# Hybrid trunk: the second query tile loaded and split ahead of the second HGRN, its loads and query factors in other places

## The chip, the cores and the metric

The kernel runs on one core of a Trainium2 chip. The time is that of one execution on the device in microseconds (us), median of several runs. The engines are TensorE (PE in the profile, its weight loads PEld), VectorE (DVE), ScalarE (ACT), GpSimd (POOL) and SyncE (SP), which issues all DMAs of this kernel. Each engine works through its own queue in order; semaphores tie them together.

## The reference

Two layers over x, 1024 tokens by 1024 columns, all in float32:

```
h = rms_norm(x);  z = h @ w_in[l]        # 2560 columns, split among three mixers
o_att = attention(q_a, k_a, v_a)         # 8 query heads, 2 key/value heads of 64, QK norm, rotary
o_hg  = hgrn2_bidirectional(...)         # 4 heads with 64 x 64 state, gated recurrence both ways
o_cv  = conformer_conv(a_c, g_c)         # gated, depthwise, 31 taps, layer norm, swish
x = x + concat[o_att, o_hg, o_cv] @ w_out[l]
x = x + relu(rms_norm(x) @ w1[l])^2 @ w2[l]
```

Attention is softmax(q k^T / 8) v without a mask, over all 1024 keys.

## The kernel before, in words

The kernel is written as one long Python program against a tile framework. The framework allots buffers (`tmp` has 4, `x8` has 8, PSUM banks `c`, `e` have 2 each and `S` 2 pairs), adds the semaphores, and orders the instructions of each engine: it goes by the order in which the code is written, but lets an instruction go ahead where its own estimate says that an earlier one isn't ready. So a statement that is moved can also move its neighbours. All arrays stand with columns on partitions and tokens along the free axis. Products need more precision than one fp32r pass, so operands are split into a rounded part and a remainder (ACT copies, DVE or POOL subtracts) and multiplied in three passes.

Within a layer, the mixers run interleaved. A projection of one 128-column tile is `dense_steps` (L227): 48 matmuls of 128x512 into a pair of `S` banks, then an evacuation by DVE (`evac`, L329 and L331). The weights come through `wtile`: a load to `raw` (L200), ACT's copy to `whi` (L203), the remainder to `wlo` by DVE, or by POOL for w_out (L204). First come the convolution's inputs and the first HGRN half (`Hgrn(0)`) with the q, k and v projections (`qkv`); normed and rotated queries and keys go out to DRAM as `qd` and `kd`. The queries' norm factors are only multiplied in later, by `query_norm(j)`, for all but the first of four: it loads 512 KB of qd, widens the factors `nqc` over the tokens (ACT, L172, into a `tmp` buffer), turns them by PE transposes (L182), multiplies (DVE, L676) and stores.

Then the attention's first steps are woven into the second HGRN half, `h1 = Hgrn(1, mid)`: its constructor does five projections (q, two forget gates, the output gate, and the value i), and `mid` is called ahead of the last. Its output gate is stored to DRAM (`gd`, L443), and its core is a generator, `gen`, advanced inside the attention loop. In the same projections ends the convolution (`cg`), whose outputs go to `mixd` (L409).

Attention goes over 16 query tiles `w` (head h, half of the tokens: 512 queries). For one tile:
- `att_query(w)` loads 64 rows of qd twice (L769, two DMAs of 128 KB), copies them on ACT (L774, L775) and subtracts the remainder (L777; on DVE for tile 0, on POOL for the others);
- `att_max(w, i)`, i = 0 to 3: two matmuls of 128x512 against the keys (L785) and two reductions to row maxima on DVE (L788);
- `att_shift(w)`: the maxima of the halves are joined (L791), transposed (L793) and put into the query tile (L794), so that the second pass of the scores subtracts them;
- `att_scores(w, i)`: eight score matmuls by pairs (L807, L808) and the Exp on ACT (L809);
- `att_values(w)`: 64 matmuls (L819) and the division (L827, L828); `att_out(w)` transposes (L841).

`keys(g)` loads and splits the keys of one kv head (L751 to L757). The pool `att` holds the query tiles `Q`, the probabilities `PT` and outputs, and lies in the space that `xs`, the normed input of the projections, frees when the last projection has been read.

## Time and profile before

| | us |
|---|---|
| median of 3 runs | 2493.56 (2493.47 to 2499.18) |
| profiled execution | 2494.11 |
| its span, first to last instruction | 2492.3 |
| PE busy | 2403.3 |
| DVE, ACT, POOL busy | 1832.8, 1070.0, 553.6 |
| mean granted clock of TensorE | 0.982 |

The last projection of the second HGRN ends at about 301 us in layer 0 and 1544 us in layer 1, and the attention loop follows to about 530 and 1773. A timeline row shows the start, the time (of the whole row, where it merges xN instructions), engine, line and operation, and in brackets the idle time before it with what ended it. A row of waits shows who waited for whom, the sum, how often, and the longest.

### The profile page before, as it was taken

How to read it: one execution, taken by the hardware profiler on the slowest of the kernel's cores; microseconds unless marked ns; L12 is line 12 of the kernel's file. 1: busy time of each engine (PE TensorE's matmuls, PEld its weight loads, DVE VectorE, ACT ScalarE, POOL GpSimd, SP SyncE). 2: the span in 40 equal slices, each digit the busy share in tenths (PEclk: the TensorE clock that was granted, in tenths of full speed). 3: DMA queues.
4: the chain of work that ended last, by engine and by line, in shares of the span. 5: the costliest groups of instructions: out<-in, count | busy, mean ns of one | idle time of the engine just before them, and what ended most of it. 6: DMA issues, size and time to landing. Idle time of an engine off the chain costs nothing. (4 is left out here: it accounts for less than half of the span.)

```text
span 2492.3 us, 40044 instructions
## 1 busy us (share of the span) xinstructions
PE 2403.3 (96%) x16192; PEld 1925.2 (77%) x16192; DVE 1832.8 (74%) x2747; ACT 1070.0 (43%) x1616; POOL 553.6 (22%) x305
## 2 busy tenths in 40 slices
PE   8989899999999999999999898999999999999999
PEld 7767667778788887888887676677787888878887
DVE  6998486633977768987859974865349776789886
ACT  5233455543544444433523234555435444444332
POOL 0251432013035420000123424310130354100000
PEclk9999999999999999999999889999999999999999
DMA  4111321042344458444221123210423444574442
GB/s 159 59 35 65 103 81 36 10 153 81 118 151 146 162 178 295 150 172 161 70 101 49 35 73 106 69 36 10 153 85 120 151 162 147 200 270 163 149 152 93
DMA packets 114825, 293.45 MB, mean 118 GB/s; under 512 B 11600, under 2 KB 11984, under 8 KB 114640
## 3 DMA queue, kind: packets, MB, share of 16 engines
q1 hardware_dynamic: 114640, 290.90, 33.4%
q8 instruction: 127, 2.08, 0.3%
q14 instruction: 58, 0.48, 0.1%
HBM read 200.67 MB, written 90.18 MB: 117 GB/s over the span
## 5 line engine op out<-in xcount | busy, mean ns | idle before, releaser
L227 PE MATMUL S<-xs,whi 128*128 128x512 f32 x1280 | 364.1, 404 | 8.4 <-ACT whi L203 7.0
L227 PEld LDWEIGHTS S<-xs,whi 128*128 128x128 f32 x1280 | 242.0, 192 | 62.9 <-ACT whi L203 7.0
L788 DVE TENSOR_REDUCE mq<-c 128x1 f32<-128x512 f32 x256 | 170.5, 685 | 48.1 <-PE c L785 44.0
L1255 PE MATMUL S<-xs,xs 128*128 128x512 f32 x816 | 201.7, 390 | 2.6 <-DVE xs L956 2.6
L227 PE MATMUL S<-xs,wlo 128*128 128x512 f32 x640 | 202.1, 397 | 0.0
L955 ACT ACTIVATE xs<-m 128x512 fp32r<-128x512 f32 x216 | 126.0, 619 | 141.9 <-DVE m L966 50.8
L809 ACT ACTIVATE PT<-S 128x1024 f32<-128x1024 f32 x128 | 128.3, 1023 | 126.1 <-PE S L808 77.8
L1255 PEld LDWEIGHTS S<-xs,xs 128*128 128x128 f32 x816 | 152.9, 188 | 35.5 <-DVE xs L956 3.5
L361 DVE SCALAR_TENSOR_TENSOR x<-x,par,x 128x1014 f32<-128x1014 f32 (+14 forms) x120 | 161.6, 1381 | 0.0
L956 DVE TENSOR_TENSOR xs<-m,xs 128x512 fp32r<-128x512 f32 x216 | 144.8, 693 | 22.5 <-ACT xs L955 22.5
L203 ACT ACTIVATE whi<-raw 128x1024 fp32r<-128x1024 f32 x56 | 59.1, 1057 | 208.4 <-PE S L227 181.5
L227 PEld LDWEIGHTS S<-xs,wlo 128*128 128x128 f32 x640 | 122.4, 192 | 26.3
L819 PEld LDWEIGHTS e<-x,PT 128*64 128x64 f32 x4096 | 124.8, 138 | 22.1 <-issue 9.9
L1255 PE MATMUL e<-xs,xs 128*128 128x512 f32 x552 | 140.8, 390 | 1.0 <-ACT xs L955 0.6
L1255 PE MATMUL c<-xs,xs 128*128 128x512 f32 x552 | 139.2, 389 | 0.0
L819 PE MATMUL e<-x,PT 128*64 128x65 f32 x4096 | 131.4, 223 | 7.6 <-DVE Q L794 3.9
L265 POOL TENSOR_TENSOR tmp<-tmp,tmp 128x1024 f32<-128x1024 f32 x19 | 50.8, 2673 | 363.2 <-ACT tmp L264 363.0
L227 PE MATMUL S<-mx,whi 128*128 128x512 f32 x448 | 122.9, 396 | 0.0
L1255 PEld LDWEIGHTS e<-xs,xs 128*128 128x128 f32 x552 | 103.3, 188 | 24.2 <-DVE xs L956 1.4
L553 POOL TENSOR_TENSOR X<-X,T 128x512 f32<-128x512 f32 x56 | 99.5, 1796 | 96.9 <-ACT m L494 47.2
L1255 PEld LDWEIGHTS c<-xs,xs 128*128 128x128 f32 x552 | 103.6, 188 | 21.5
L785 PE MATMUL c<-x,Q 128*128 128x512 f32 x240 | 101.7, 456 | 14.6 <-POOL Q L777 13.7
(311 smaller groups left out, 5229.1 us busy)
## 6 DMA issues: line engine op xcount, KB each, us to landing
m<-ad SPq DMA_DIRECT2D x104, 512.0 KB, 3.9
ad<-x SPq DMA_DIRECT2D x176, 256.0 KB, 2.2
raw<-w_in_t SPq DMA_DIRECT2D x40, 512.0 KB, 3.3
xs<-w_t SPq DMA_DIRECT2D x36, 512.0 KB, 3.7
raw<-w_t SPq DMA_DIRECT2D x36, 512.0 KB, 3.4
m<-w_t SPq DMA_DIRECT2D x32, 512.0 KB, 6.7
ad<-tmp SPq DMA_DIRECT2D x48, 256.0 KB, 2.2
x<-w_t SPq DMA_DIRECT2D x24, 512.0 KB, 5.0
```

The lines of the kernel that those rows point to most:

```text
L203: nc.scalar.activation(hi, raw, AF.Copy)
L227: nc.tensor.matmul(zp[h] if type(zp) is list else zp[:, h, :], w, xx[:, h * 512 : (h + 1) * 512], start=first, stop=last)
L265: return i, eng.tensor_tensor(self.ssq, self.ssq, sq, op=ALU.add)
L361: nc.vector.scalar_tensor_tensor(y[:, lo:hi], u[:, lo + d : hi + d], par[:, l, wof + tap : wof + tap + 1], y[:, lo:hi], op0=ALU.mult, op1= ...
L553: eng.tensor_tensor(xv, xv, tv, op=ALU.mult)
L785: nc.tensor.matmul(b, QS[w][:, 0, i * P : (i + 1) * P], KH[g][:, hb * 512 : (hb + 1) * 512], start=True, stop=True)
L788: nc.vector.tensor_reduce(MX[w][:, hb, i : i + 1], b, axis=AX.X, op=ALU.max)
L809: nc.scalar.activation(PT[w][:, 2 * i : 2 * i + 2, :], s, AF.Exp)
L819: nc.tensor.matmul(pvp[64 * b : 64 * b + 64, i * 65 : (i + 1) * 65], PT[w][:, kb, q0 : q0 + 64], VS[g][:, kb, 0:65], start=kb == 0, stop=k ...
L955: ordered("a", nc.scalar.activation(hi, src, AF.Copy))
L956: ordered("v", nc.vector.tensor_tensor(lo, src, hi.bitcast(F32), op=ALU.subtract))
L1255: nc.tensor.matmul(banks[dt], w[i][:, dt * P : (dt + 1) * P], a[j], start=n == 0 and name not in ("M6", "M7", "M3"), stop=n == 3 * SG - 1, ...
```

## The change

`att_query(1)` now stands right after `keys(0)`, ahead of the second HGRN, with an `x8` buffer and the subtraction on DVE, as tile 0 has it. `mid` does all four steps of tile 0's maxima ahead of the value projection, no longer two of them. The loads of tiles 2 and up go into two buffers `qq` of their own, in the `att` pool, no longer into `tmp`. The first shift is written ahead of tile 2's load. In the loop, the load of tile w + 3 moves from the head of a pass behind its second scores, and the query factors of passes 0, 2 and 6 behind its fourth.

```diff
         def att_query(w):
             h, half = quads[w]
-            qq = tmp((P, 512))
+            qq = tmp((P, 512)) if w < 2 else ap_.t([P, 512], "qq", bufs=2)
...
-            q = x8((P, 2, 512), dt=F32R) if w == 0 else ap_.t([P, 2, 512], "Q", bufs=4, dt=F32R)
+            q = x8((P, 2, 512), dt=F32R) if w < 2 else ap_.t([P, 2, 512], "Q", bufs=4, dt=F32R)
...
-            eng = nc.gpsimd if w > 0 else nc.vector
+            eng = nc.gpsimd if w > 1 else nc.vector
...
         att_query(0)
         keys(0)
-        h1 = Hgrn(1, lambda: (att_max(0, 0), att_max(0, 1)))
+        att_query(1)
+        h1 = Hgrn(1, lambda: [att_max(0, i) for i in range(4)])
...
         nc.vector.memset(mxw, 0.0)
-        att_query(1)
-        att_max(0, 2)
-        att_max(0, 3)
+        att_shift(0)
         att_query(2)
-        att_shift(0)
...
             if w == 2:
                 keys(1)
-            if w in (0, 2, 6):
-                query_norm((w + 2) // 4 + 1)
-            if w + 3 < NQ:
-                att_query(w + 3)
             for i in range(4):
...
                 if i == 1 and w > 1:
                     att_out(w - 2)
+                if i == 1 and w + 3 < NQ:
+                    att_query(w + 3)
+                if i == 3 and w in (0, 2, 6):
+                    query_norm((w + 2) // 4 + 1)
```

What it does to the engines' queues is the same in both layers; the rows are those of layer 0. In the names `x_259` is query tile 0 (`x_265` tile 1 after), `x_262` and `x_263` are the keys, `c` and `S` PSUM banks.

PE, in the last projection of the second HGRN, before:

```order
L785 MATMUL c_2317<-x_262_1962,x_259_1954 128x512
L227 MATMUL S_314_2333<-xs_103,whi_2132 128x512 x2
L227 MATMUL S_314_2333<-xs_104,whi_2132 128x512 x2
L227 MATMUL S_314_2333<-xs_103,wlo_2133 128x512 x2
L227 MATMUL S_314_2333<-xs_108,whi_2132 128x512 x2
L785 MATMUL c_2320<-x_262_1962,x_259_1954 128x512
L227 MATMUL S_314_2333<-xs_109,whi_2132 128x512 x2
L785 MATMUL c_2323<-x_262_1962,x_259_1954 128x512
```

and after:

```order
L785 MATMUL c_2331<-x_262_1962,x_259_1954 128x512
L227 MATMUL S_321_2353<-xs_108,wlo_2141 128x512
L785 MATMUL c_2334<-x_262_1962,x_259_1954 128x512
L227 MATMUL S_321_2353<-xs_108,wlo_2141 128x512
L227 MATMUL S_321_2353<-xs_113,whi_2140 128x512
L785 MATMUL c_2337<-x_262_1962,x_259_1954 128x512
L227 MATMUL S_321_2353<-xs_113,whi_2140 128x512
L227 MATMUL S_321_2353<-xs_114,whi_2140 128x512
L785 MATMUL c_2340<-x_262_1962,x_259_1954 128x512
```

The second four maxima matmuls of tile 0 follow the first four inside the projection, with one or two of its matmuls between them.

PE, from the end of that projection to the first finished scores (L808), before:

```order
L785 MATMUL c_2397<-x_262_1962,x_259_1954 128x512
L785 MATMUL c_2400<-x_262_1962,x_259_1954 128x512
L807 MATMUL S_336_2447<-x_259_1954,x_262_1962 128x512
L807 MATMUL S_339_2459<-x_259_1954,x_262_1962 128x512
L785 MATMUL c_2403<-x_262_1962,x_259_1954 128x512
L785 MATMUL c_2406<-x_262_1962,x_259_1954 128x512
L785 MATMUL c_2453<-x_262_1962,Q_2392 128x512
L785 MATMUL c_2456<-x_262_1962,Q_2392 128x512
L785 MATMUL c_2465<-x_262_1962,Q_2392 128x512
L793 MATMUL e_2418<-cons_77,mxw_2387 128x128
L182 MATMUL e_2425<-cons_77,tmp_2423 128x128 x4
L785 MATMUL c_2468<-x_262_1962,Q_2392 128x512
```

and after:

```order
L807 MATMUL S_329_2422<-x_259_1954,x_262_1962 128x512
L785 MATMUL c_2428<-x_262_1962,x_265_1970 128x512
L785 MATMUL c_2431<-x_262_1962,x_265_1970 128x512
L807 MATMUL S_332_2434<-x_259_1954,x_262_1962 128x512
L785 MATMUL c_2440<-x_262_1962,x_265_1970 128x512
L793 MATMUL e_2410<-cons_77,mxw_2407 128x128
L182 MATMUL e_2487<-cons_77,tmp_2485 128x128 x4
L785 MATMUL c_2443<-x_262_1962,x_265_1970 128x512
L808 MATMUL S_329_2422<-x_259_1954,x_263_1963 128x512
```

The four matmuls against tile 1 stay ahead of L808, but read the tile that was split ahead of the HGRN; of the two sets of four transposes (L182) one is left there, the other stands behind the first two scores.

ACT, around the same place, before:

```order
L440 ACTIVATE mx_2309<-tmp_2307 128x1
L172 ACTIVATE tmp_2423<-nqc_784 128x1024
L203 ACTIVATE whi_5109<-raw_5107 128x1024
L774 ACTIVATE Q_2392<-tmp_2389 64x512
L775 ACTIVATE Q_2392<-tmp_2389 64x512
L774 ACTIVATE Q_2412<-tmp_2409 64x512
L775 ACTIVATE Q_2412<-tmp_2409 64x512
L774 ACTIVATE Q_2441<-tmp_2438 64x512
L775 ACTIVATE Q_2441<-tmp_2438 64x512
L809 ACTIVATE PT_2446<-S_336_2447 128x1024
```

and after:

```order
L440 ACTIVATE mx_2317<-tmp_2315 128x1
L172 ACTIVATE tmp_2485<-nqc_784 128x1024
L203 ACTIVATE whi_5109<-raw_5107 128x1024
L774 ACTIVATE Q_2416<-qq_2413 64x512
L775 ACTIVATE Q_2416<-qq_2413 64x512
L774 ACTIVATE Q_2449<-qq_2446 64x512
L809 ACTIVATE PT_2421<-S_329_2422 128x1024
```

Ahead of the first Exp stand three query copies in place of six, now those of tiles 2 and 3 out of `qq`; the widened factors (L172) keep their place.

## The prediction

> **What bounds the kernel now.** I read the page's engine lines first, then the waits of TensorE (PE) in the attention stage of each layer (289 to 520 us and 1520 to 1790 us), then the timelines of PE, ScalarE (ACT), GpSimd (POOL) and VectorE (DVE) around the longest wait. PE carries the kernel:

> ```profile
> span 2492.3 us, 40044 instructions
> PE 2403.3 (96%) x16192; PEld 1925.2 (77%) x16192; DVE 1832.8 (74%) x2747; ACT 1070.0 (43%) x1616; POOL 553.6 (22%) x305
> ```

> PE stands still for 89 us in all, so an edit to the order can gain only there. The longest wait of either attention stage is one and the same place, POOL's split of query tile 1 (L777), once in each layer:

> ```profile
> PE c L785 <- POOL Q L777: 7.2, 1, 7.2
> ...
> PE c L785 <- POOL Q L777: 6.5, 1, 6.5
> ```

> The PE timeline of layer 0 shows it between the last projection of the second HGRN (its last rows start at 300.79) and the first finished scores (L808):

> ```profile
> 299.89 1.07 PE L227 MATMUL S<-xs,whi 128*128 128x512 f32 x4
> 300.79 0.62 PE L227 MATMUL S<-xs,wlo 128*128 128x512 f32 x2
> 301.25 0.62 PE L785 MATMUL c<-x,x 128*128 128x512 f32 x2
> ...
> 302.73 0.50 PE L807 MATMUL S<-x,x 128*128 128x512 f32 x1 [0.64 <-DVE m L331]
> 303.41 1.09 PE L785 MATMUL c<-x,x 128*128 128x512 f32 x2 [0.18 <-DVE mq L788]
> 311.74 1.22 PE L785 MATMUL c<-x,Q 128*128 128x512 f32 x2 [7.24 <-POOL Q L777]
> ...
> 315.41 0.72 PE L182 MATMUL e<-cons,tmp 128*128 128x128 f32 x4
> 315.88 0.48 PE L808 MATMUL S<-x,x 128*128 128x512 f32 x1
> ```

> POOL isn't the root. It waited for ACT, and ACT for a store:

> ```profile
> 293.43 0.21 ACT L440 ACTIVATE mx<-tmp 128x1 f32<-128x1 f32 x1
> 305.93 1.05 ACT L172 ACTIVATE tmp<-nqc 128x1024 f32<-128x1024 f32 x1 [12.29 <-DMA gd<-tmp]
> 306.89 1.04 ACT L203 ACTIVATE whi<-raw 128x1024 fp32r<-128x1024 f32 x1
> 307.83 0.61 ACT L774 ACTIVATE Q<-tmp 64x512 fp32r<-64x512 f32 x1
> ...
> 316.85 1.95 ACT L809 ACTIVATE PT<-S 128x1024 f32<-128x1024 f32 x2 [1.02 <-PE S L808]
> ...
> 308.01 2.34 POOL L204 TENSOR_TENSOR wlo<-raw,whi 128x1024 fp32r<-128x1024 f32 x1 [5.86 <-ACT whi L203]
> 310.43 2.49 POOL L777 TENSOR_TENSOR Q<-tmp,Q 64x512 fp32r<-64x512 f32 x2
> ```

> L172 widens the query factors into a tmp buffer that the gate's store still read; ACT is in order, so the weight split (L203) and the query copies (L774) stood behind it, and on POOL the 2.34 us weight split ahead of the query's. After the wait PE also ran slowly: two L785 rows took 1.22 us, where four L227 rows took 1.07. The granted clock (the column before the last two) says why:

> ```profile
> 306.00:308.00 2.00, 0.00 (x0) 0.00 (x0) 0.00 (x0) 2.00 (x3) 0.00 (x0) 0.50 0.12 47
> ...
> 316.00:318.00 2.00, 2.00 (x12) 1.45 (x10) 2.00 (x4) 1.15 (x2) 1.21 (x1) 1.00 0.00 0
> ```

> So the place costs more than the 7.24 us of waiting.

> **The change, priced in layer 0.** Query tile 1 and the second half of tile 0's maxima go ahead of and into the projections.

> *Early load and split.* SP gets two 128 KB loads ahead of three w_out loads, ACT two copies (0.63 us each), DVE one subtraction (0.69), POOL loses one. They sit where these engines are idle:

> ```profile
> 256.05 0.69 DVE L777 TENSOR_TENSOR x<-tmp,x 64x512 fp32r<-64x512 f32 x1 [0.63 <-ACT x L775]
> ...
> 262.35 1.06 ACT L203 ACTIVATE whi<-raw 128x1024 fp32r<-128x1024 f32 x1 [1.56 <-PE S L227]
> ...
> 262.80 1.22 DVE L331 TENSOR_TENSOR tmp<-S,Rb 128x1024 f32<-128x1024 f32 x1 [1.71 <-PE S L227]
> ...
> DMA to landing us min/median/max: 2.4/2.8/5.9
> ```

> The load reuses the tmp buffer that DVE frees at 256.74 and lands at 259.6 by the median, so both copies fit in ACT's 1.56 us: nothing. At the longest landing (5.9, at 262.7) DVE's evacuation L331, behind the split, would be 1.9 us late and PE's next transposes up to 1 us: bounds 0 and 1.0; I take 0, the median. The w_out loads behind them are some 2 us later; their splits on ACT stand behind the end of the next projection, so nobody waits. SP passes nothing else.

> *Four maxima moved into the projection.* PE's work is the same; L227's pace is (1.07 - 0.39) / 3 = 0.227 us, so the projection ends 4 x 0.227 = 0.91 later, at 302.16. Their reduces fall into DVE idle time:

> ```profile
> 290.78 2.74 DVE L788 TENSOR_REDUCE mq<-c 128x1 f32<-128x512 f32 x4
> ...
> 301.45 1.23 DVE L331 TENSOR_TENSOR m<-S,Rb 128x1024 f32<-128x1024 f32 x1 [7.92 <-PE S L227]
> 302.73 2.51 DVE L788 TENSOR_REDUCE mq<-c 128x1 f32<-128x512 f32 x4
> ```

> Four more fill 2.5 of the 7.92 us. With two banks the reduce pace of 0.61 bounds the maxima, and PE has one or two matmuls between them: 0 to 0.4 us of waits; I take 0.

> *From the projection's end to the first scores.* The evacuation ends 302.73 - 301.25 = 1.48 after PE's last row: 303.64. Then DVE does two reduces of tile 1 (0.61 + 0.69, to 304.94) and the shift L794 (0.68), so L808 can start at 305.7. Before it was 315.88: 10.2 us ahead. Four transposes of the factors come later instead (0.72 at half clock, some 0.4): 9.8 net. That needs L172 early. In the changed program its buffer is no longer the gate's but that of the second conv output, stored by L409 when POOL is done at 296.2. With the landings below it runs from 299.4, and its transposes are due at 304.9.

> ```profile
> 293.82 2.39 POOL L408 TENSOR_TENSOR tmp<-tmp,x 128x1024 f32<-128x1024 f32 x1
> ...
> mixd<-tmp SPq DMA_DIRECT2D x3, 512.0 KB, 3.2
> tmp<-qd SPq DMA_DIRECT2D x10, 128.0 KB, 3.2
> ```

> *What is late next.* The query tiles 2 and 3 now load into the space that xs frees at the projection's end. SP waits there (behind it only a w_out load, a store and keys(1)'s loads), issues at 302.4 and 303.5 behind the gate's 512 KB store; with a landing of 3.2 and an estimated 0.4 for that store the tiles are there at 306.0 and 307. ACT has their copies in order ahead of the first Exp: 306 + 3 x 0.63 gives an Exp at 307.9 where the scores would allow 306.7 (before, the first Exp at 316.85 stood 0.97 behind L808). That takes back 0.6 (landing at the 2.8 median) to 1.2; I take 0.9. DVE owes 0.68 us (an L553 that now comes after the maxima); it is the third busy time in this row, 9.53 of 10 us, so that counts, and an estimated 0.4 more for the factor multiplies (L676) that now stand ahead of the second value product.

> ```profile
> 350.00:360.00 10.00, 9.18 (x164) 7.04 (x155) 9.53 (x15) 6.60 (x10) 4.07 (x3) 1.00 0.25 80
> ```

> Layer 0: 9.8 - 0.9 - 0.7 - 0.4 = 7.8 us. Up to the first value product (335.76 before) both orders hold the same PE work, so nothing else is owed there.

> *The queries and factors inside the loop* only change places by a few Exps; their loads follow POOL's split two tiles back, over a whole pass of the loop earlier than ACT's copy: 0, bounded by +-1 us a layer.

> *Layer 1* is the same order, with a shorter wait: 1553.79 - 1546.23 = 7.56 against 8.33 from 303.41 to 311.74. So 7.0.

> ```profile
> 1546.23 1.09 PE L785 MATMUL c<-x,x 128*128 128x512 f32 x2 [0.18 <-DVE mq L788]
> 1553.79 1.22 PE L785 MATMUL c<-x,Q 128*128 128x512 f32 x2 [6.47 <-POOL Q L777]
> ```

> After the attention stage no instruction changes place, and PE is full there; the shift goes through to the end. Sum: 7.8 + 7.0 = 14.8 us off the profiled execution's 2494.11, 2479.3; the median of the runs shown is 0.55 lower, so 2478.8.

> **The clock.** Between 302.2 and 305.7 PE will still wait three or four times, 0.1 to 0.8 us each. Short waits can cost clock too: in layer 0 a wait of 1.64 us is followed by half clock, in layer 1 the same wait is not. Between these rows layer 0 takes 137.44 us and layer 1 135.84, so one such dip costs 1.6 us:

> ```profile
> 376.06 0.33 PE L819 MATMUL e<-x,PT 128*64 128x65 f32 x2 [1.64 <-DVE Q L794]
> ...
> 513.50 3.95 PE L819 MATMUL e<-x,PT 128*64 128x65 f32 x128 [0.41 <-DVE tmp L629]
> ...
> 1619.33 0.33 PE L819 MATMUL e<-x,PT 128*64 128x65 f32 x2 [1.64 <-DVE Q L794]
> ...
> 1755.17 3.95 PE L819 MATMUL e<-x,PT 128*64 128x65 f32 x128 [0.41 <-DVE tmp L629]
> ...
> 378.00:379.00 1.00, 1.00 (x4) 0.66 (x2) 0.00 (x0) 0.83 (x1) 0.00 (x0) 0.50 0.00 0
> ```

> I leave the sum alone and put 1.6 us a layer into the range, to both sides, since layer 0's dip may go. [...]

> **Rivals.** (1) *L172 still holds ACT.* If the gate's store (with 0.9 later projection, 306.8) or another transfer holds it, its transposes run at 307.9, the scores at 308.7, L203 and the copies push the first Exp to 311.4, against 316.85 before: 5.4 ahead, less 1.1 of DVE's debt, 4.3 a layer, 2485. For it: 12.29 us, the longest ACT wait here. Against: the buffer named above. (2) *Attention is bound by DVE and gives most back.* Between 316 and 376 PE waits for DVE or ACT in many short pieces; if half of what is won goes into them, 3.9 + 3.5 leaves 2486.5, no change that can be told. Against: DVE is early too, it saves 7.33 us of idle time and four reduces in the same place:

> ```profile
> 312.57 0.69 DVE L788 TENSOR_REDUCE mq<-c 128x1 f32<-128x512 f32 x1 [7.33 <-PE c L785]
> ```

> (3) *Slower: the loop's query copies hold ACT's Exps.* qq has two buffers where tmp had four; if each of the 26 later loads were late for its copy, every us of lateness would count, since the copy stands ahead of Exps in order. The gain is eaten at 14.8 / 26 = 0.57 us each; at 1.2 us each the time is 2494.1 + 26 x 1.2 - 14.8 = 2510. For it: the copies of tiles 2 and 3 are late above for just this reason. Against: from then on a load waits for a split two passes back, and a pass takes about 13 us (fifteen of them from 315.88 to 513.50).

> **How the numbers follow.** A change under 0.3% (7.5 us) can't be told from none. My case: 0.80, with 2473 (both layers the full 9.8 and 9.0 and layer 0's dip gone: 2494.1 - 20.4, less 0.55) to 2483 (a dip in each layer and 1 us each for the late load). Rival 1: 0.06; rival 2: 0.09; rival 3: 0.05. The range goes up to 2487, which takes in rivals 1 and 2. Rival 1 counts as faster: faster 0.86, within 0.3% 0.09, slower 0.05; I move 0.02 to the middle, since rival 1 lies on the edge.

> **What would show it.** Right: no PE wait for L777 above 1 us, all eight first maxima beside L227, L808 4 to 5 us after the projection's end (14.6 before), L172 at about 299, granted clock 1.00 from 306 to 316. Wrong: L172 or a query copy on ACT behind a DMA while PE waits for Exps, or PE waits for DVE between 316 and 376 that grow by more than 3 us a layer.

## The result, and the profile after

The changed kernel takes 2477.67 us (median of 4 runs, 2475.13 to 2478.92), the kernel before 2494.72 beside it: ratio 0.9928, 95% interval [0.9915, 0.9942]. The forecast was 2478.8. The engine lines of the changed kernel's page:

```profile
span 2475.3 us, 40059 instructions
PE 2394.3 (97%) x16192; PEld 1920.8 (78%) x16192; DVE 1841.1 (74%) x2749; ACT 1070.2 (43%) x1616; POOL 550.1 (22%) x303
```

PE has as many matmuls as before. It is busy 9.0 us less and idle 8.0 us less (5.7 and 11.0 in the second run of the same program, below). It is busy for less time because it has less time at half clock, where two rows of L785 took 1.22 us (311.74 before) and not 0.61 (303.07 below): the mean granted clock is 0.988 for 0.982. In the list of waits L777 no longer stands on PE's side. What PE waits for at that place, between 300 and 312 us, is small (engine, what it waited for, sum, times, longest), and layer 1 has the same three waits:

```profile
PE e L793 <- DVE mxw L791: 0.7, 1, 0.7
PE S L807 <- DVE m L331: 0.6, 1, 0.6
PE c L785 <- DVE mq L788: 0.2, 1, 0.2
```

The PE timeline from the end of the projection to the first scores in layer 0:

```profile
302.39 0.61 PE L227 MATMUL S<-xs,wlo 128*128 128x512 f32 x2
302.84 0.39 PE L807 MATMUL S<-x,x 128*128 128x512 f32 x1
303.07 0.61 PE L785 MATMUL c<-x,x 128*128 128x512 f32 x2
304.32 0.50 PE L807 MATMUL S<-x,x 128*128 128x512 f32 x1 [0.64 <-DVE m L331]
305.00 0.49 PE L785 MATMUL c<-x,x 128*128 128x512 f32 x1 [0.18 <-DVE mq L788]
306.16 0.33 PE L793 MATMUL e<-cons,mxw 128*128 128x128 f32 x1 [0.67 <-DVE mxw L791]
306.33 0.60 PE L182 MATMUL e<-cons,tmp 128*128 128x128 f32 x4
306.76 0.50 PE L785 MATMUL c<-x,x 128*128 128x512 f32 x1
...
307.36 0.50 PE L808 MATMUL S<-x,x 128*128 128x512 f32 x1
```

And ACT beside it:

```profile
301.08 1.06 ACT L172 ACTIVATE tmp<-nqc 128x1024 f32<-128x1024 f32 x1 [6.94 <-DMA mixd<-tmp]
302.58 1.06 ACT L203 ACTIVATE whi<-raw 128x1024 fp32r<-128x1024 f32 x1 [0.45 <-PE S L227]
306.35 0.63 ACT L774 ACTIVATE Q<-qq 64x512 fp32r<-64x512 f32 x1 [2.70 <-DMA qq<-qd]
...
308.36 1.94 ACT L809 ACTIVATE PT<-S 128x1024 f32<-128x1024 f32 x2
```

L172 waits for the conv output's store, not for the gate's, and the three pieces of PE's waiting there are short. Later places of the same engine, to be set beside the same rows of before in the prediction, carry the account:

```profile
368.71 0.33 PE L819 MATMUL e<-x,PT 128*64 128x65 f32 x2 [1.66 <-DVE Q L794]
...
503.71 3.95 PE L819 MATMUL e<-x,PT 128*64 128x65 f32 x128 [0.41 <-DVE tmp L629]
...
520.22 2.27 PE L819 MATMUL e<-x,PT 128*64 128x65 f32 x44 [2.47 <-issue]
...
1542.93 0.50 PE L808 MATMUL S<-x,x 128*128 128x512 f32 x1
...
1604.20 0.33 PE L819 MATMUL e<-x,PT 128*64 128x65 f32 x2 [1.64 <-DVE Q L794]
...
1739.25 3.95 PE L819 MATMUL e<-x,PT 128*64 128x65 f32 x128 [0.41 <-DVE tmp L629]
```

Against 376.06, 513.50, 1619.33 and 1755.17 the changed kernel is ahead by 7.35, 9.79, 15.13 and 15.92 us. Its profiled execution was 0.5 us late ahead of everything that the change moves (the PE row of L227 that starts at 245.25 before starts at 245.76), and 6.78 us ahead when layer 1's second HGRN began (1520.61 against 1513.83). So layer 0 gives 7.85 us up to the first row, the first shift of the loop, and 10.3 up to the second; layer 1 gives 8.35 and 9.1 up to the same two places.

### The profile page after: what moved, and what is told of

Read it like the earlier page. It is cut to its first block, busy times and chain, and to the rows that moved or that the text cites. A ratio compares the mean times of both kernels' runs of the same rounds, so it can differ in the third digit from the quotient of the medians.

```text
span 2475.3 us, 40059 instructions
## 1 busy us (share of the span) xinstructions
PE 2394.3 (97%) x16192; PEld 1920.8 (78%) x16192; DVE 1841.1 (74%) x2749; ACT 1070.2 (43%) x1616; POOL 550.1 (22%) x303
## 4 chain that ended last, share of the span: by engine, by line
PE 82%; DVE 15%; issue 2%; POOL 1%; ACT 1%; DMA 0%; SPq 0%; DVEq 0%; ACTq 0%; POOLq 0%
PE S L227 17%; PE S L1253 10%; PE c L1052 10%; PE S L1052 7%; PE e L1052 7%; PE e L1253 7%; PE c L1253 7%; PE e L819 4%; DVE x L361 4%; PE S L807 2%; PE c L785 2%; PE S L808 2%; PE e L612 1%; DVE mq L788 1%; PE e L504 1%
## 5 line engine op out<-in xcount | busy, mean ns | idle before, releaser
L227 PE MATMUL S<-xs,whi 128*128 128x512 f32 x1280 | 363.6, 404 | 8.9 <-ACT whi L203 7.6
L227 PEld LDWEIGHTS S<-xs,whi 128*128 128x128 f32 x1280 | 241.6, 192 | 62.5 <-ACT whi L203 7.6
L227 PE MATMUL S<-xs,wlo 128*128 128x512 f32 x640 | 202.6, 397 | 0.0
L788 DVE TENSOR_REDUCE mq<-c 128x1 f32<-128x512 f32 x256 | 169.7, 684 | 29.7 <-PE c L785 25.8
L809 ACT ACTIVATE PT<-S 128x1024 f32<-128x1024 f32 x128 | 128.0, 1024 | 122.8 <-PE S L808 74.3
L203 ACT ACTIVATE whi<-raw 128x1024 fp32r<-128x1024 f32 x56 | 59.1, 1057 | 206.0 <-PE S L227 179.2
L227 PEld LDWEIGHTS S<-xs,wlo 128*128 128x128 f32 x640 | 122.1, 191 | 26.2
L819 PEld LDWEIGHTS e<-x,PT 128*64 128x64 f32 x4096 | 124.9, 138 | 21.9 <-issue 9.7
L819 PE MATMUL e<-x,PT 128*64 128x65 f32 x4096 | 131.5, 224 | 7.9 <-DVE Q L794 3.9
L553 POOL TENSOR_TENSOR X<-X,T 128x512 f32<-128x512 f32 x56 | 100.2, 1811 | 106.6 <-ACT m L494 54.2
L227 PE MATMUL S<-mx,whi 128*128 128x512 f32 x448 | 123.7, 398 | 0.0
L807 PE MATMUL S<-Q,x 128*128 128x512 f32 x224 | 94.6, 422 | 6.2 <-ACT PT L809 6.2
## 6 DMA issues: line engine op xcount, KB each, us to landing
m<-ad SPq DMA_DIRECT2D x104, 512.0 KB, 3.9
raw<-w_in_t SPq DMA_DIRECT2D x40, 512.0 KB, 3.3
xs<-w_t SPq DMA_DIRECT2D x36, 512.0 KB, 3.6
raw<-w_t SPq DMA_DIRECT2D x36, 512.0 KB, 3.5
m<-w_t SPq DMA_DIRECT2D x32, 512.0 KB, 6.6
x<-w_t SPq DMA_DIRECT2D x24, 512.0 KB, 4.9
```

The costliest lines, as they stand in the source:

```text
L203: nc.scalar.activation(hi, raw, AF.Copy)
L227: nc.tensor.matmul(zp[h] if type(zp) is list else zp[:, h, :], w, xx[:, h * 512 : (h + 1) * 512], start=first, stop=last)
L553: eng.tensor_tensor(xv, xv, tv, op=ALU.mult)
L788: nc.vector.tensor_reduce(MX[w][:, hb, i : i + 1], b, axis=AX.X, op=ALU.max)
L807: nc.tensor.matmul(s[:, n, :], KH[g][:, ks], QS[w][:, 0], start=True, stop=False)
L809: nc.scalar.activation(PT[w][:, 2 * i : 2 * i + 2, :], s, AF.Exp)
```

## The experiments

Theory: the gain comes from taking tile 1's split and ACT's L172 off PE's path at the projection's end. Rivals: one part alone does it (the early split, the maxima inside the projection, the moves in the loop). The table has, of each profiled execution, when L172, the first L808 and the first Exp of layer 0 start, and by how much that execution was already late at 250 us, ahead of everything that the kernels change ("late", against the execution of before; it is to be taken off the three times).

| kernel | late | L172 | L808 | first Exp | median us | ratio to before |
|---|---|---|---|---|---|---|
| before |  | 305.93 | 315.88 | 316.85 | 2494.7 | |
| changed | 0.5 | 301.08 | 307.36 | 308.36 | 2477.7 | 0.9928 [0.9915, 0.9942] |
| changed, again | 0.7 | 301.11 | 307.53 | 308.52 | 2477.4 | 0.9936 [0.9924, 0.9949] |
| before + early tile 1 | 1.0 | 301.92 | 310.06 | 311.72 | 2482.5 | 0.9953 [0.9938, 0.9968] |
| before + four maxima | 0.3 | 306.19 | 313.74 | 315.40 | 2488.7 | 0.9977 [0.9968, 0.9987] |
| before + loop moves | 0.6 | 307.88 | 310.83 | 312.35 | 2486.1 | 0.9962 [0.9949, 0.9976] |
| changed, loads in tmp | 1.2 | 306.43 | 308.26 | 310.94 | 2480.9 | 0.9947 [0.9933, 0.9960] |
| changed, loop moves undone | 0.3 | 300.66 | 307.56 | 308.53 | 2475.8 | 0.9931 [0.9916, 0.9945] |
| changed, two maxima | 2.0 | 302.33 | 310.10 | 311.42 | 2478.2 | 0.9938 [0.9926, 0.9950] |
| shift in projection | 3.1 | 302.28 | 307.81 | 308.69 | 2481.1 | 0.9949 [0.9937, 0.9961] |
| one-input L791 | 0.8 | 301.51 | 306.74 | 308.51 | 2472.8 | 0.9912 [0.9900, 0.9925] |
| shift in, one-input | 0.8 | 300.66 | 303.60 | 304.48 | 2473.2 | 0.9914 [0.9901, 0.9927] |
| the same, loop undone | 0.8 | 300.65 | 304.44 | 305.35 | 2475.4 | 0.9918 [0.9903, 0.9933] |

**Tile 1 early, alone.**

```diff
-            q = x8((P, 2, 512), dt=F32R) if w == 0 else ap_.t([P, 2, 512], "Q", bufs=4, dt=F32R)
+            q = x8((P, 2, 512), dt=F32R) if w < 2 else ap_.t([P, 2, 512], "Q", bufs=4, dt=F32R)
...
-            eng = nc.gpsimd if w > 0 else nc.vector
+            eng = nc.gpsimd if w > 1 else nc.vector
...
+        att_query(1)
         h1 = Hgrn(1, lambda: (att_max(0, 0), att_max(0, 1)))
...
-        att_query(1)
         att_max(0, 2)
```

> The kernel before (2494.7 us) with one part of the change alone: tile 1 loaded and split ahead of the second HGRN; two maxima in the projection, loads in tmp and the loop as before. Theory (the gain comes from L172 no longer holding ACT behind the gate's store): in this order L172's buffer is one that POOL's gate product frees, so it runs at about 301 and not 305.9; the scores L808 start at about 307 (315.88 before), the first Exp a little later than in the changed kernel because tile 3's load now waits for the gate's store: 2481 (2478 to 2484). Rival 1 (what counts is that tile 1's split leaves POOL, wherever L172 stands): the same or a little better, 2479. Rival 2 (what counts is the maxima inside the projection): at most half of the gain, 2486 or more.

0.9953: two thirds of the gain (4.7 of 7.2 thousandths). This run frees L172 and takes tile 1's split off POOL at once, so it cannot tell the theory from rival 1; the runs with the loop moves alone and with L172 held again, below, take the two one at a time. L172 came at the time expected, L808 2 us later than expected (310.06 less 1.0). A part of that is PE's half clock from 305.7 on: the two sets of four transposes (L182) ahead of L808 take 1.06 us each, where a set takes 0.60 in the changed kernel. Three stretches of this run (PE busy first, granted clock third from the end):

```profile
302.30:305.70 3.40, 2.30 (x8) 0.89 (x6) 3.29 (x6) 2.77 (x4) 2.51 (x2) 1.00 0.85 282
305.70:309.10 3.40, 3.21 (x9) 2.12 (x10) 3.00 (x5) 0.00 (x0) 1.94 (x2) 0.50 0.13 47
309.10:312.50 3.40, 3.40 (x12) 2.79 (x11) 3.28 (x6) 2.04 (x3) 0.84 (x1) 0.50 0.89 293
```

The first two of these stretches in the changed kernel:

```profile
302.30:305.70 3.40, 2.38 (x9) 1.17 (x7) 2.66 (x4) 1.06 (x1) 2.33 (x2) 1.00 0.70 239
305.70:309.10 3.40, 2.84 (x14) 2.15 (x15) 3.40 (x6) 2.63 (x4) 1.69 (x2) 1.00 0.80 231
```

PE was busy for 2.30 us of the first stretch in the one, 2.38 in the other; only behind the first did the clock fall. Busy time alone doesn't tell which.

**Four maxima, alone.**

```diff
-        h1 = Hgrn(1, lambda: (att_max(0, 0), att_max(0, 1)))
+        h1 = Hgrn(1, lambda: [att_max(0, i) for i in range(4)])
...
         att_query(1)
-        att_max(0, 2)
-        att_max(0, 3)
         att_query(2)
```

> The kernel before (2494.7 us) with all four maxima of tile 0 in the projection and nothing else. Theory: L172 is still held by the gate's store to about 306.8, tile 1's split is as late as before, PE still waits 7 us or more for L777: 2494 (2491 to 2497). Rival 1: 2494 too. Rival 2 (the maxima): about half of the gain, 2486.

0.9977, a gain of 6 us where none was expected. The median, 2488.7, lies outside the theory's range (2491 to 2497) and nearer to rival 2. L172 is still held (306.19), but PE's wait for L777 is 4.06 us, not 7, and L808 is 2.4 ahead: the shift (L793) and a set of transposes now come ahead of that wait. The profiled execution is the slowest of its 12 (2493.88), so it doesn't show where the median's 6 us lie.

**The moves in the loop, alone.**

```diff
-            if w in (0, 2, 6):
-                query_norm((w + 2) // 4 + 1)
-            if w + 3 < NQ:
-                att_query(w + 3)
...
+                if i == 1 and w + 3 < NQ:
+                    att_query(w + 3)
+                if i == 3 and w in (0, 2, 6):
+                    query_norm((w + 2) // 4 + 1)
```

> The kernel before (2494.7 us) with the moves inside the loop alone (query factors behind the fourth scores, loads behind the second); tile 1 still loaded late and split on POOL behind the weight split, two maxima in the projection. Theory (head of the line on ACT): L172 now stands behind the copies of tiles 1 to 3, so L203 runs at 301.4, the copies from 302.4, POOL's weight split ends at 305 and tile 1's split at 306.3 (311.7 before); PE still waits some 2 us for it, L808 starts at about 308.3, 7.6 ahead: 2481 (2479 to 2484). Rival 1 (tile 1 has to leave POOL): the wait for L777 stays above 4 us with half clock behind it, 2488 to 2494. Rival 2: 2494.

0.9962. The chain does what the theory says: L172 goes behind the copies, and PE's wait for L777 falls to 1.40 us although tile 1 is split by POOL after the projection. L808 is 5.6 us ahead, not 7.6, again at half clock (the set of L182 ahead of it takes 1.06 us), and the median, 2486.1, lies between the theory's range (to 2484) and rival 1's (from 2488). So an edit that frees the head of ACT's line, and leaves tile 1's split on POOL behind the weight split, brings half of the gain.

**The changed kernel with L172 held again.**

```diff
-            qq = tmp((P, 512)) if w < 2 else ap_.t([P, 512], "qq", bufs=2)
+            qq = tmp((P, 512))
```

> The changed kernel (2477.7 us) with the loads of tiles 2 and up back in tmp. Tile 2 and 3 then load early, but L172's tmp buffer is again the one that the gate's store reads. Theory: L172 is held to about 307, its transposes stand ahead of L808 on PE, which starts at about 309 (307.4 in the changed kernel), L203 and the copies push the first Exp to about 311 (308.4): 2 to 3 us a layer are lost, 2483 (2481 to 2485). Rival 1 (tile 1's early split alone counts): no loss, 2478. Third view (the late loads into the space of xs cost 0.9 us a layer): 2476.

This is the prediction's rival 1 made real. The gate's store holds L172 as before, and with it the Exps:

```profile
306.43 1.05 ACT L172 ACTIVATE tmp<-nqc 128x1024 f32<-128x1024 f32 x1 [11.64 <-DMA gd<-tmp]
...
310.94 1.94 ACT L809 ACTIVATE PT<-S 128x1024 f32<-128x1024 f32 x2
```

0.9947: 3.2 us above the changed kernel's median, 1.6 a layer, less than the 2 to 3 expected and less than the rival's price (2485). In the traces the first Exp is 1.9 later, less what each was late, and at the places of 513.50 and 1755.17 the lead over before is 7.3 and 6.3 us, where the changed kernel has 10.3 and 9.1: 2.9 a layer, as expected, of which waits and dips elsewhere give a part back. L808 itself is only 0.25 later, so the loss comes after it; the loads of the loop stand in `tmp` too in this run, and what these cost is not told apart. The two parts replace each other: the early tile with L172 free but the other parts missing, the loop moves, and this kernel each have half to three quarters of the gain, and the first two together (12.1 + 8.6 us) would be more than the whole.

**The changed kernel again, and without single parts.** The first is the same program, the second has the loop of before, the third this:

```diff
-        h1 = Hgrn(1, lambda: [att_max(0, i) for i in range(4)])
+        h1 = Hgrn(1, lambda: (att_max(0, 0), att_max(0, 1)))
...
+        att_max(0, 2)
+        att_max(0, 3)
         att_shift(0)
```

> The changed kernel again, for a second trace and more runs. Theory (the waits of PE for tile 1 and the half clock behind it are gone for good; the rest of the layer varies with things the change doesn't touch): 2477.7 (2475.5 to 2480); L808 at 307 to 307.5 and full clock from 305.7 to 316 again in both layers; PE's unexplained wait in the last value product of a layer (2.47 us in layer 0 and none in layer 1 of the first trace, 1.10 and 1.17 in the kernel before) takes other values, 0 to 2.5. Rival (the result hangs on where the 3.4 us windows of the clock fall): a half-clock window at 302 to 316 in one layer, 1.7 us each, and a median up to 2481.

> The changed kernel with the moves inside the loop undone (query factors and loads at the head of a pass again). L172 keeps a buffer that the second conv output frees, so it still runs at 301. Theory (the moves inside the loop are worth 0 +-1 us a layer once L172 is free): 2478 (2476 to 2480). Rival (the loop moves carry the gain, as they brought 8.6 us by themselves): 2486.

> The changed kernel with two of tile 0's four maxima steps in the projection, the other two behind it. Theory: L172 runs at 301 as in the changed kernel; the four reduces (2.5 us) stand ahead of the shift on DVE again, the projection ends 0.9 earlier, so L808 comes 1.6 us later at full clock; PE's window 302.3 to 305.7 is emptier (about 0.6 busy, as in the run with the early tile alone), so 3.4 to 6.8 us of half clock may follow, 1.7 to 3.4 more in a layer: 2482 (2479.5 to 2487). Rival (the maxima in the projection bring nothing): 2478.

Again 2477.4, with the first scores at the same place at full clock in both layers; two half-clock stretches stand later in layer 1 (1586 and 1596 us; mean granted clock of the execution 0.986), and PE's unexplained wait was 1.48 us in layer 0 and 0.82 in layer 1 (2.47 and none in the first trace). Without the loop moves 0.9931: they are worth nothing that can be told once L172 has another buffer, as expected. With two maxima 0.9938, which can't be told from the changed kernel either: the expectation (2482) was wrong, though in layer 0 of the trace L808 comes 1.2 us later and 3.4 us are at half clock (granted clock 0.78 from 305.7 to 309.1 and 0.72 from there to 312.5); in layer 1 L808 is 0.5 later, at full clock.

**The shift inside the projection.**

```diff
-            nc.tensor.transpose(b[:, 0:P], mxw, ident)
+            nc.tensor.transpose(b[0:64, 0:P], mxw, ident)
...
-        h1 = Hgrn(1, lambda: [att_max(0, i) for i in range(4)])
+        mxw = cst.t([P, 64], "mxw")
+        nc.vector.memset(mxw, 0.0)
+
+        def mid():
+            for i in range(4):
+                att_max(0, i)
+            att_shift(0)
+
+        h1 = Hgrn(1, mid)
...
-        mxw = ap_.t([P, P], "mxw")
-        nc.vector.memset(mxw, 0.0)
-        att_shift(0)
         att_query(2)
```

> The changed kernel with tile 0's shift inside the projection too (behind its maxima; its buffer mxw is 64 columns wide and lies in a pool that is open all along). PE then needs nothing of DVE after the projection, L808 can start at about 303.5 instead of 307.4, and the program's order has two Exps ahead of tile 2's copies. Theory (PE's waits at this place are what is left to win): up to 3.9 us a layer at the first scores, of which DVE, busy 9.5 of 10 us up to 360, leaves about half: 2474 (2470 to 2477). Rival (DVE bounds the stretch from 316 to 376 by itself): 2477.5, no gain.

0.9949: no gain, rather a loss of some 3 us, which neither view expected. PE now stood still within the projection, for an L791 that is 0.15 us long where POOL is idle; PE, DVE and POOL in that order:

```profile
301.77 0.27 PE L793 MATMUL e<-cons,mxw 128*64 128x128 f32 x1 [1.84 <-DVE mxw L791]
```

```profile
299.30 2.32 DVE L791 TENSOR_TENSOR mxw<-mq 128x4 f32<-128x4 f32 x1
```

```profile
299.26 2.35 POOL L204 TENSOR_TENSOR wlo<-raw,whi 128x1024 fp32r<-128x1024 f32 x1
```

L791 starts 0.04 us behind POOL's weight split and ends with it. In the changed kernel the same pair stands at the first shift:

```profile
303.73 2.36 POOL L204 TENSOR_TENSOR wlo<-raw,whi 128x1024 fp32r<-128x1024 f32 x1 [1.06 <-ACT whi L203]
```

```profile
304.87 1.24 DVE L791 TENSOR_TENSOR mxw<-mq 128x4 f32<-128x4 f32 x1
```

That wait does not make the loss by itself: L808 is still 2.1 us earlier than in the changed kernel, less what each was late. The lead is lost after it: the first shift of the loop, 368.71 in the changed kernel, is at 374.37 here, 3.1 later by the same reckoning, with two stretches at half clock (357 and 367 us; mean granted clock of the execution 0.984) ahead of it.

**L791 with one input.**

```diff
-            nc.vector.tensor_tensor(mxw[:, 0:4], MX[w][:, 0], MX[w][:, 1], op=ALU.max)
+            nc.vector.tensor_reduce(mxw[:, 0:4], MX[w].rearrange("p h i -> p i h"), axis=AX.X, op=ALU.max)
```

> The changed kernel (2477.5 us) with one DVE operation replaced: the maxima of the two halves (L791) are joined by a reduction over one SBUF operand instead of a maximum of two SBUF operands; same result, same place in every queue around it. In the changed kernel L791 takes 0.15 to 0.17 us when POOL is idle at its start, but each of the 14 that start while a POOL instruction runs ends 0.02 us behind that one, up to 1.24 us. Theory (two SBUF inputs on DVE wait for POOL's instruction): the reduction takes under 0.3 us everywhere, PE's wait for it ahead of the first shift (0.67 us) goes, L808 starts 1.0 to 1.1 us earlier in each layer (306.3 for 307.4): 2475.5 (2474 to 2477). Rival (L791 waits for the write of the maxima just ahead of it): it stays at 1.2 us at this place, 2477.5. [...]

0.9912, the lowest median of all (2472.83; all four runs, 2471.09 to 2474.40, lie below all nine of the changed kernel). The groups of L791, of the changed kernel and of this one (count | busy us, mean ns):

```profile
L791 DVE TENSOR_TENSOR mxw<-mq 128x4 f32<-128x4 f32 x32 | 16.8, 526 | 0.5
```

```profile
L791 DVE TENSOR_REDUCE mxw<-mq 128x4 f32<-128x8 f32 x32 | 5.0, 156 | 0.5
```

It takes 156 ns in the mean, and 0.15 us at 305.21, in the middle of POOL's L204 (304.07 to 306.43); again 14 of the 32 start while a POOL instruction runs. L808 starts at 306.74 in an execution that was 0.3 us later: 1.0 earlier. That is the theory. The medians differ by 4.6 us, more than the 2 expected, but the other 13 that POOL had held did not bring the rest: the lead over the changed kernel is 1.0 a layer at L808 and 1.1 a layer at the first shift and at the loop's end, 2.3 in all. What is beyond that lies in half clock (mean granted clock 0.989 for 0.988) and in the unexplained wait (1.42 us in layer 0 and none in layer 1), which differ between two runs of one program too, so it is not shown to be the edit's.

**Both together, with and without the loop moves.**

> The kernel with the shift inside the projection (2481.1 us), with the one-input reduction for L791. There PE's transpose waited 1.84 us in the middle of the projection for an L791 of 2.32 us, which ended with POOL's weight split. Theory (that lock took the gain of the earlier shift): the wait falls below 0.4 us, L808 starts 1.9 us earlier than there; against the changed kernel the first scores are some 3 us ahead, of which DVE's work leaves a part: 2473.5 (2469 to 2476.5). Rival (DVE bounds the stretch up to 376 by itself, or the transpose stands too early for another reason): 2477 to 2480.

> The same, with the moves inside the loop undone. The loop moves showed no cost and no gain once L172 is free (2475.8 without them, 2477.4 with them): 2473 (2469 to 2477), no difference from the kernel above. Rival (tile 2's copies now stand between the first two Exps on ACT and the factors' transposes ahead of L808 on PE): 1 us a layer later, 2475.

L791's wait for POOL was what had cost the earlier shift (0.9949 to 0.9914); all 32 are changed at once, so which of them counted stays open. Against the one-input kernel nothing is won: 0.9914 and 0.9918 for 0.9912. Without the loop moves L808 comes 0.8 later, as the rival there said, but the medians can't be told apart. With the shift inside, the first scores come 3.1 us earlier than in the one-input kernel, and PE stands still later. The stretches 303 to 310 and 340 to 350, first of the one-input kernel, then with the shift inside (PE busy first, DVE third):

```profile
303.00:310.00 7.00, 5.68 (x26) 3.81 (x25) 6.57 (x12) 4.28 (x6) 4.28 (x2) 1.00 0.79 229
...
340.00:350.00 10.00, 9.04 (x161) 7.47 (x160) 9.53 (x16) 3.83 (x7) 2.68 (x2) 1.00 0.18 65
```

```profile
303.00:310.00 7.00, 6.97 (x33) 4.90 (x31) 6.43 (x9) 5.93 (x8) 5.03 (x3) 1.00 0.70 228
...
340.00:350.00 10.00, 8.30 (x156) 6.94 (x150) 9.90 (x16) 4.85 (x8) 4.06 (x3) 1.00 0.22 80
```

PE gains 1.3 us in the first and loses 0.7 in the second, where DVE is busy for 9.90 of 10. At the first shift of the loop 0.4 of the 3.1 us are left in layer 0, behind a half-clock stretch at 360 us, and nothing in layer 1 (1599.19 against 1597.84, where this execution began layer 1's second HGRN 1.4 later), which has none. So the prediction's rival 2, which did not happen to this change, does happen to the next one; that it is DVE's work which takes the lead is argued from its busy time, not tested.

## Why the prediction was right

The mechanism held: no PE wait for L777, the maxima beside L227, full clock from 305.7 on, L808 4.5 us behind the projection's end. The single terms held less well than their sum. By the prediction's own steps, times less the 0.5 us by which this execution was late:

- *Early load and split, 0:* right. The copies fit ahead of L203, which waited 0.27 us for PE and was not late, and DVE's evacuation follows 0.03 us behind the split:

```profile
262.62 0.69 DVE L777 TENSOR_TENSOR x<-tmp,x 64x512 fp32r<-64x512 f32 x1 [0.90 <-ACT x L775]
263.34 1.22 DVE L331 TENSOR_TENSOR tmp<-S,Rb 128x1024 f32<-128x1024 f32 x1
```

- *Moved maxima, +0.91 and 0 of waits:* the projection ended 1.1 later, so 0.2 of waits, inside the bound of 0.4.
- *L808 at 305.7:* mis-sized; 306.9. The sum had L791 at nothing. It took 1.24 us here, behind POOL's L204, and the run with one input put it right (306.74 less the 0.84 it was late: 305.9). The lead at L808 is 9.0 in layer 0 and 8.4 in layer 1 (1542.93 against 1558.13, less 6.78). L172 was due at 299.4 and ran at 300.6, which cost nothing.
- *Late copies, 0.9, and DVE's debt, 0.7 and 0.4:* the times of the copies were right (copy due at 306.0, ran at 305.85; first Exp due at 307.9, came at 307.86), but the sum charges 1.6 of this up to the first value product, and there (the first row is of before, the second of the changed kernel) the lead is 10.0 us in layer 0 and 9.5 in layer 1: nothing had been taken. The two times 0.4 in these sums, for the gate's store and for the factor multiplies, were estimates, which no run shows singly.

```profile
335.76 1.27 PE L819 MATMUL e<-x,PT 128*64 128x65 f32 x36
...
326.29 1.27 PE L819 MATMUL e<-x,PT 128*64 128x65 f32 x36
```

In the one-input run L808 comes 1.0 earlier, the first Exp only 0.2, and the first shift still 1.1, so the late Exp does not hold that place. The lead shrinks only after the first value product: by 2.1 us in layer 0 and 1.1 in layer 1 up to the first shift, where the sum had 0.4.
- *Layer 0, 7.8, and layer 1, 7.0, up to there:* 7.85 and 8.35. That layer 0 comes out to 0.05 us is luck: the terms stand at other places than they were put. Layer 1 is 1.35 above its term, and 1.0 of that is a wait of the kernel before that the term left out. In its layer 1 the second query copy (L775) waited for its load, so the Exp behind it and PE came 1.0 later there than at the same place of layer 0:

```profile
343.49 0.50 PE L807 MATMUL S<-Q,x 128*128 128x512 f32 x1 [0.54 <-ACT PT L809]
...
1586.76 0.50 PE L807 MATMUL S<-Q,x 128*128 128x512 f32 x1 [1.54 <-ACT PT L809]
```

```profile
341.76 0.63 ACT L775 ACTIVATE Q<-tmp 64x512 fp32r<-64x512 f32 x1
...
1585.03 0.63 ACT L775 ACTIVATE Q<-tmp 64x512 fp32r<-64x512 f32 x1 [0.92 <-DMA tmp<-qd]
```

- *The queries and factors inside the loop, 0 with a bound of 1:* between the first shift and the loop's last value products the changed kernel gains 0.8 us in both layers, half clock apart; the kernel without the loop moves does not, but it is 0.35 and 1.6 further ahead at the shift. That leaves 0.5 and -0.8, inside the bound.
- *Rivals:* rival 1 was built (2480.9, still a gain). Rival 2 did not happen: 2.1 of 10.0 and 1.1 of 9.5 us of the lead were given back, not half. Rival 3 did not happen either: ACT waits for a load into `qq` once in each layer, 2.7 us at tile 2's copy, and for none of the loads in the loop.
- *The clock, 1.6 a layer in the range:* layer 0's dip behind the wait of 1.66 us is gone (granted clock 1.00 from 366 to 372). Of the 2.4 us won in that stretch 0.8 are the loop's, as in layer 1, so the dip was worth 1.6. PE's wait at 520.22, 2.47 us and half clock behind it (0.50 from 520.7 to 524.1) where before has 1.10 us, took 2.9 back: layer 0 ends at 7.4. In layer 1 before has such a wait too (1.17) and the changed kernel none: 9.1 becomes 10.5. The second trace of the same program has other values, so I count these as chance and not as the change's.

The sum: -0.5 + 7.4 - 0.1 between the layers + 10.5 - 0.3 after = 17.0 us of span, where 14.8 were forecast. Of the 2.2 between them, 1.0 is the late load in layer 1 of before and 1.6 the two layers' 0.8 in the loop; the rest is the balance of dips and waits. So a forecast within 1.1 us of the median owes something to errors that cancel. Two smaller slips of the prediction: an edit to the order can gain not only in PE's 89 us of idle time, since 9.0 of the 17.0 us came out of its busy time; and a dip in each layer with 1 us each for the late load adds up to 2484, not 2483. What PE's wait in the last value product is stays open: the profile names no releaser.

## What to carry to other kernels

When an engine stalls a long way down a chain, look for the instruction at the head of an in-order queue and for the transfer that holds its buffer: giving L172 another place was worth 8.6 us by itself, but freeing it by another buffer brought only 3.2 more once the work that it delayed had been moved. Such parts don't add up. After such a stall is gone, read the shortest instructions on the new path at their longest, not at their mean; a 0.15 us operation that took 1.24 was the next thing to win. Before moving work still earlier, see which engine is full behind it, or the gain may be given back there. And when the gain differs between two layers of one program, look at what differs between them in the kernel before.

## What the runs showed of the hardware

L791, a DVE maximum of two SBUF operands of 128x4 elements, ends 0.02 us behind the POOL instruction that runs when it starts: 14 of 14 in the changed kernel, which take up to 1.24 us (2.32 with the shift inside the projection). The other 18, which start with POOL idle, take 0.15 to 0.17. With one input the 32 take 156 ns in the mean, and the one at 305.21, in the middle of POOL's L204, takes 0.15.

```profile
350.00:353.40 3.40, 1.69 (x9) 1.23 (x10) 3.40 (x6) 2.23 (x4) 2.66 (x2) 1.00 0.27 77
353.40:356.80 3.40, 3.40 (x45) 2.48 (x43) 3.21 (x6) 3.38 (x5) 0.00 (x0) 1.00 0.00 0
```

The half clock of the changed kernel starts at 117.9, 158.9, 213.5 and 520.7 us (among others), 41.0, 54.6 and 307.2 apart; divided by 12, 16 and 90 that is 3.41 each. What brings such a stretch on, the runs don't show.
